# Row sums in two rounded parts, group sums in halves, and the last row tile's closing steps in another order

## The chip, the cores and the metric

The kernel runs on one core of a Trainium2 chip. The core has a matrix engine (TensorE, PE in the profile; its weight loads are PEld), three engines for element-wise work (VectorE or DVE, ScalarE or ACT, GpSimd or POOL) and a queue that issues most of the transfers (SyncE, SP). The metric is the device time of one execution in microseconds, as a median over runs.

## The reference

One layer of a hybrid network on a sequence of 2048 tokens with 1024 features, in float32:

```
mod = silu(c) @ w_ada + b_ada
shift_m, scale_m, gate_m, shift_f, scale_f, gate_f = split(mod, 6)
h = adaln(x, g_norm_mix, shift_m, scale_m)
p = h @ w_in                      # 1024 -> 3592, split into conv, q, k, v, z, a, b
ya = group_rms_norm(gate_b * conv(gate_c * h_conv))       # 8 groups of 64
yb = rms_norm(gated_delta_rule(q, k, v, g, beta)) * silu(z)
x = x + gate_m * (concat(ya, yb) @ w_out)
h = adaln(x, g_norm_ffn, shift_f, scale_f)
gt, up = split(h @ w_gate_up, 2)
x = x + gate_f * ((silu(gt) * up) @ w_down)
shift_o, scale_o = split(silu(c) @ w_ada_final + b_ada_final, 2)
out = adaln(x, g_norm_final, shift_o, scale_o)
```

`adaln(x, gain, shift, scale)` is `rms_norm(x) * gain * (1 + scale) + shift`. `rms_norm` divides by the root of the mean square over the features; the group norm does so over groups of 64.

## The kernel before

**Products in three parts.** To keep float32 accuracy the kernel splits nearly every operand of a matmul into a rounded part (hi, type F32R, "fp32r" in the profile) and the rounded rest (lo), and computes hi·hi, hi·lo and lo·hi into the same bank. These dense matmuls of 128 x 512 are recorded under L322. A weight strip arrives by DMA in a tile `wraw` (a ring of four), ACT casts it to `whi` (L389), DVE subtracts to get `wlo` (L391), and three strips are kept ready ahead. The strip then serves 24 dense matmuls.

**Stages.** The adaLN vectors and the first normalisation come first, then the mixer in four blocks of 512 tokens (from about 133, 400, 640 and 925 us of the span), then the gate and up products (about 1100 to 1950), and then the down products to the end. In each mixer block PE runs the projections, and in between them the small matmuls of the convolutions, of the delta rule and of the norms. These are written as generators, which `dmm` (L322) resumes as the dense matmuls go on.

**PSUM.** Dense results go to a pool `pd` of four banks. All side work takes its bank from another pool of four, `pm`, by `misc_ps()`. A generator that takes a bank before the engines have read its old content makes the next writer wait.

**The order.** A class `Clock` keeps planned times for each engine while the program is built, and decides by them when a generator is resumed. In the mixer it also sorts each engine's queue by the planned begin times and pins that order. So an edit in one place can move instructions in the whole block.

**Rows of adaLN (`to_row`, L502).** A vector such as gate_m is accumulated as products over 128 partitions in `acc`, a tile of the weight ring. The bias is added on DVE (L505), and a matmul with a matrix of ones sums over the partitions and spreads the row to all of them (L510), in halves of 512 columns. In the mixer (`mixing[0]`) this matmul takes `acc` unrounded, in float32; PE needs two passes per half, and the profile counts them as two matmuls. This happens twice: for gate_m in block 0, where `put` copies the half to a tile, and for gate_f in block 2, where `put` copies it on ACT (L498) and stores it by DMA (L499). After the mixer the other branch is used, which rounds first.

**Group sums (`mix_chain`, L1294).** For the group norm the squares of a 128 x 512 tile are split into `sh` and `sl`, and two matmuls with a matrix of group ones (L1307, L1308) sum them in one bank. This happens four times per block, 16 times in all.

**The closing stage (loop over `items`, L1855).** An item is one row tile pair `s` with one group of weights. The down products use Strassen's scheme: per item A11B11, S1T1, A12B21, S2T2 and S4B22, and, in the middle of the next item, the two late products p7 (S3T3) and p4 (A22T4) of the item before. `add` (L1812, DVE) adds a bank to an accumulator of 128 x 1024. With the last group, `finish` (L1815 to L1829) normalises a finished accumulator: `sum_squares` (ACT L536, POOL L530 and L531, a power), then per half a scaling on ACT to a `pm` bank (L1824), a product with go on DVE (L1825), an addition of so on POOL (L1826), and a store (L1829). The last accumulator goes through `finish_last` (L1832 to L1851), which does its halves apart around p4. The names `acc_1_16433`, `acc_0_16478` and `acc_1_16480` below are the second accumulator of the item before the last (row tile 14 in the text on the prediction), and the first and second of the last item. In the new program they are `acc_1_16481`, `acc_0_16526` and `acc_1_16528`.

Of the kernel before, what the change touches and what calls it, by code (L numbers as in the profile page):

```python
# [12 lines left out]
F32 = mybir.dt.float32  # L13
# [197 lines left out]
def layer_kernel(ctx, tc, x, c, w_ada, b_ada, w_ada_final, b_ada_final, g_norm_mix, g_norm_ffn, g_norm_final,  # L211
# [22 lines left out]
    def misc_ps():  # L234
        return pm.tile([P, 512], F32, name="pm")
# [238 lines left out]
    def settled(*tiles):  # L474
        yield
        yield
        while clock.pinned and due(tiles, 0) + 2 > clock.pe:
            yield
# [23 lines left out]
    def to_row(acc, bias_row, put):  # L502
# [1 line left out]
        nc.sync.dma_start(brow, bias_row)  # L504
        nc.vector.tensor_add(acc[0:1, :], acc[0:1, :], brow)  # L505
        if mixing[0]:
            yield from settled(acc)
            for ns in (slice(n * 512, (n + 1) * 512) for n in range(2)):
                ps = misc_ps()
                mm(ps, ones, acc[:, ns], start=True, stop=True)  # L510
                put(ns, ps)
            return
        hi, lo = temp(F32R), []
        clock.kept.add(hi.name)
# [206 lines left out]
    with ExitStack() as actx:  # L721
# [144 lines left out]
        for b in range(NB):  # L866
# [428 lines left out]
            def mix_chain(m, cv):  # L1295
# [8 lines left out]
                nc.vector.tensor_sub(sl, sy, sh.bitcast(F32))  # L1304
                yield sh, sl
                ps = misc_ps()
                mm(ps, gones_r, sh, start=True, stop=False)  # L1307
                mm(ps, gones_r, sl, start=False, stop=True)  # L1308
                give("lv", 2)
                nc.scalar.activation(sy, ps, AF.Sqrt, scale=1.0 / 64, bias=epsc)  # L1310
                nc.vector.reciprocal(sy, sy)
# [499 lines left out]
    def add(s, u, ns, ps):  # L1811
        nc.vector.tensor_add(accs[s, u][:, ns], accs[s, u][:, ns], ps)  # L1812

    def row(s, u):
        r = s // CH * 8 + u * CH + s % CH  # L1815
        return slice(r * P, (r + 1) * P)
# [12 lines left out]
        nc.sync.dma_start(out[row(s, u), :], t)  # L1829


    def finish_last(s, u):  # L1832
        a, go, so = accs[s, u], fin["go_d"], fin["so_d"]
        m = dp.tile([P, D], F32, name="T")[:, h0]
        s2 = [g0.tile([P, 1], F32, name="ss", bufs=4) for _ in range(2)]
        junk = sp.tile([P, D], mybir.dt.bfloat16, name="ht", bufs=2)
        nc.scalar.activation(junk[:, h1], a[:, h1], AF.Square, accum_out=s2[1])
        nc.gpsimd.tensor_mul(a[:, h1], a[:, h1], go[:, h1])  # L1838
        nc.vector.tensor_scalar(s2[1], s2[1], 1.0 / D, EPS, op0=ALU.mult, op1=ALU.add)
        yield  # L1840
        nc.scalar.activation(junk[:, h0], a[:, h0], AF.Square, accum_out=s2[0])
        nc.vector.tensor_mul(m, a[:, h0], go[:, h0])
        nc.vector.scalar_tensor_tensor(s2[0], s2[0], 1.0 / D, s2[1], op0=ALU.mult, op1=ALU.add)
        nc.gpsimd.tensor_tensor(s2[0], s2[0], mhalf[:, :1], op=ALU.pow)
        c0, c1 = slice(0, 256), slice(256, 512)
        nc.scalar.activation(a[:, c1], m[:, c1], AF.Identity, scale=s2[0])
        nc.gpsimd.tensor_add(a[:, c1], a[:, c1], so[:, c1])
        nc.vector.scalar_tensor_tensor(a[:, h1], a[:, h1], s2[0], so[:, h1], op0=ALU.mult, op1=ALU.add)  # L1848
        nc.vector.scalar_tensor_tensor(a[:, c0], m[:, c0], s2[0], so[:, c0], op0=ALU.mult, op1=ALU.add)
        for h in (h1, h0):  # L1850
            nc.sync.dma_start(out[row(s, u), h], a[:, h])  # L1851

    load_pair(1)
    late = None
    for n, (g, s) in enumerate(items):  # L1855
# [33 lines left out]
        next(ahead, None)  # L1889
        dproduct(b, parts("A12", "B21"), True)  # L1890
        add(s, 0, h0, b)
        work()
        dproduct(a, parts("S2", "T2"), False)
        add(s, 0, h1, a)
# [2 lines left out]
        dproduct(c_, parts("S4", "B22"), False)  # L1897
        add(s, 0, h1, c_)
        work()
        if g == last:  # L1900
            spawn(finish(s, 0), 1)
        if late:
            late[1]()
        work()

# [4 lines left out]
        def p4(a=a, s=s, q=parts("A22", "T4"), g=g):  # L1910
            dproduct(a, q, False)
            add(s, 1, h0, a)
            if g == last and s < 2 * CH - 1:
                spawn(finish(s, 1), 1)

        late = p7, p4
    late[0]()
    end = finish_last(2 * CH - 1, 1)
    next(end)
    late[1]()  # L1920
    for _ in end:
        pass
    drain()


# [18 lines left out]
```

## Time and profile before

| | |
|---|---|
| median of 3 runs | 2406.51 us (2406.47 to 2407.99) |
| span of the profiled execution | 2404.1 us |
| the profiled execution's own time | no other than its span |
| mean granted TensorE clock | 0.993 |
| PE / DVE / ACT / POOL busy | 97% / 74% / 44% / 24% |
| HBM traffic | 142 GB/s |

All of the profile is of one execution, and times in it count from the start of its span. A row of an engine's timeline gives start, duration, engine, line and operation, output <- inputs, the shape, and how many instructions the row joins; in square brackets stands the idle time just before it, with what ended it. Consecutive matmuls overlap in such rows, so the cost of one is read from start to start. In the busy times by stretch the granted clock is a share of full speed. Of the waits, a row says which line waited for which, with the sum, the count and the longest.

### The profile page before, as it was taken

To read this page: it belongs to the slowest core of one execution; us is meant where nothing else is said; L and a number is where in the kernel's file an instruction comes from. 1 tells how busy PE (TensorE), PEld (TensorE's weight loads), DVE (VectorE), ACT (ScalarE), POOL (GpSimd) and SP (SyncE) were. 2 spreads that over 40 slices of the span, in tenths; PEclk is the share of its full clock that TensorE was granted. 3 is DMA by queue.
4 is the path that set the end of the run, shared out by engine and by line. 5 is a ranking of instruction groups with operands and counts; after the bars stand their busy time and mean duration, and the time that the engine had idled before them with its cause. 6 is when DMAs were issued, how large, how long until landed. Compare 5 with 4: busy or idle time off the path is not lost. (4 is left out here: it accounts for less than half of the span.)

```text
span 2404.1 us, 30949 instructions
## 1 busy us (share of the span) xinstructions
PE 2342.0 (97%) x11285; PEld 1938.6 (81%) x11285; DVE 1779.7 (74%) x2667; ACT 1050.3 (44%) x1787; POOL 572.9 (24%) x646
## 2 busy tenths in 40 slices
PE   7899999999999999999999999999999999999997
PEld 6788888887788888887888888878888877887786
DVE  5898879775977678788666556875656568878987
ACT  3644664444634564356543334433333323322345
POOL 0241344033513161111000000000000036434448
PEclk9999999999999999999999999999999999999999
DMA  7443565535553345255663334753433374333443
GB/s 252 119 119 92 169 191 164 148 106 166 145 141 122 115 141 146 61 155 161 215 209 116 101 104 122 247 161 90 129 99 105 104 247 154 121 108 119 136 138 142
DMA packets 400992, 341.19 MB, mean 142 GB/s; under 512 B 39796, under 2 KB 343165, under 8 KB 400775
## 3 DMA queue, kind: packets, MB, share of 16 engines
q1 hardware_dynamic: 399430, 337.01, 45.9%
q0 software_dynamic: 1152, 2.10, 0.6%
q8 instruction: 88, 1.44, 0.2%
q14 instruction: 66, 0.53, 0.1%
q10 hardware_dynamic: 256, 0.10, 0.0%
HBM read 265.74 MB, written 75.51 MB: 142 GB/s over the span
## 5 line engine op out<-in xcount | busy, mean ns | idle before, releaser
L389 ACT CAST whi<-wraw 128x1024 fp32r<-128x1024 f32 x286 | 299.7, 1049 | 394.1 <-PE pd L322 170.6
L391 DVE TENSOR_TENSOR wlo<-wraw,whi 128x1024 fp32r<-128x1024 f32 x286 | 360.3, 1261 | 102.7 <-ACT whi L389 100.0
L322 PE MATMUL pd<-hTh,whi 128*128 128x512 f32 x888 | 362.0, 409 | 0.6 <-ACT hTh L564 0.6
L322 PE MATMUL pd<-hTh,wlo 128*128 128x512 f32 x888 | 348.4, 392 | 1.0 <-DVE wlo L391 1.0
L322 PE MATMUL pd<-hTl,whi 128*128 128x512 f32 x888 | 348.2, 392 | 0.1
L322 PEld LDWEIGHTS pd<-hTh,wlo 128*128 128x128 f32 x888 | 167.7, 189 | 38.2 <-DVE wlo L391 1.4
L322 PEld LDWEIGHTS pd<-hTh,whi 128*128 128x128 f32 x888 | 168.5, 190 | 33.6 <-issue 1.0
L322 PEld LDWEIGHTS pd<-hTl,whi 128*128 128x128 f32 x888 | 168.3, 190 | 32.1 <-issue 1.0
L1606 POOL TENSOR_TENSOR wraw<-wraw 128x1024 f32<-128x1024 f32 x2 | 4.9, 2458 | 776.0 <-DMA wraw<-in_w_down_dram 776.0
L1554 DVE TENSOR_TENSOR sg<-sg,pd 128x512 f32<-128x512 f32 x44 | 30.2, 686 | 163.1 <-PE pd L322 163.1
L1812 DVE TENSOR_TENSOR acc<-acc,pd 128x512 f32<-128x512 f32 x192 | 127.3, 679 | 24.6 <-PE pd L322 23.8
L1692 ACT CAST xh<-ra 128x640 fp32r<-128x640 f32 (+1 forms) x85 | 60.4, 722 | 183.0 <-PE pm L322 137.3
L1239 DVE SCALAR_TENSOR_TENSOR cv<-pd,pcb,cv 128x511 f32<-128x511 f32 (+2 forms) x173 | 129.4, 748 | 5.2
L1701 POOL TENSOR_TENSOR xl<-ra,xh 128x640 fp32r<-128x640 f32 (+1 forms) x37 | 62.7, 1695 | 143.9 <-ACT xh L1692 133.7
L1812 DVE TENSOR_TENSOR acc<-acc,pm 128x512 f32<-128x512 f32 x120 | 81.6, 680 | 17.7 <-PE pm L322 17.2
L322 PE MATMUL pd<-whi,ym 128*128 128x512 f32 x256 | 84.8, 396 | 0.0
L1741 POOL TENSOR_TENSOR wraw<-wraw 128x512 f32<-128x512 f32 x40 | 68.8, 1743 | 47.1 <-DMA wraw<-in_w_down_dram 39.7
L322 PE MATMUL pd<-A22h,whi 128*128 128x512 f32 x176 | 68.9, 391 | 3.0 <-DVE sg L1554 3.0
L322 PE MATMUL pm<-S4h,whi 128*128 128x512 f32 x176 | 68.6, 390 | 1.4 <-ACT sg L1548 1.4
L322 PE MATMUL pd<-S2h,whi 128*128 128x512 f32 x176 | 68.6, 390 | 1.0 <-ACT whi L389 1.0
L322 PE MATMUL pd<-S2h,wlo 128*128 128x512 f32 x176 | 68.6, 390 | 0.5 <-DVE wlo L391 0.5
L322 PE MATMUL pd<-S3h,t3h 128*128 128x512 f32 x176 | 69.0, 392 | 0.0
(459 smaller groups left out, 6207.2 us busy)
## 6 DMA issues: line engine op xcount, KB each, us to landing
wraw<-in_w_in_dram SPq DMA_DIRECT2D x112, 512.0 KB, 4.6
wraw<-in_w_gate_up_dram SPq DMA_DIRECT2D x88, 512.0 KB, 3.9
ra<-act SPq DMA_DIRECT2D x80, 448.0 KB, 3.6
wraw<-in_w_out_dram SPq DMA_DIRECT2D x40, 512.0 KB, 3.6
act<-S SPq DMA_DIRECT2D x80, 256.0 KB, 3.5
act<-act SPq DMA_DIRECT2D x68, 256.0 KB, 2.7
wraw<-in_w_ada_dram SPq DMA_DIRECT2D x32, 512.0 KB, 4.2
wraw<-in_w_down_dram SPq DMA_DIRECT2D x22, 512.0 KB, 4.3
```

Source lines behind the costliest of these rows:

```text
L322: mm(*args, **kw)
L389: nc.scalar.copy(hi, raw)
L391: (lo_engines.popleft() if lo_engines else nc.vector).tensor_sub(lo, raw, hi.bitcast(F32))
L1239: nc.vector.scalar_tensor_tensor(cv[:, n - t:], u[:, :BLK - n + t], taps[t], cv[:, n - t:], op0=ALU.mult, op1=ALU.add)
L1554: nc.vector.tensor_add(s5[i], s5[i], a[i])
L1606: nc.gpsimd.tensor_mul(r, r, first_w["gate"])
L1692: nc.scalar.copy(hi, raw[:, c0:c1, :])
L1701: eng.tensor_sub(lo, raw, hi.bitcast(F32))
L1741: nc.gpsimd.tensor_mul(r[:, hs], r[:, hs], gate_f[:, hs])
L1812: nc.vector.tensor_add(accs[s, u][:, ns], accs[s, u][:, ns], ps)
```

## The change

It has three parts.

1. In `to_row` in the mixer, each half of `acc` is split into hi and lo (a cast on ACT, a subtraction on DVE, both into a new tile `both` from the weight ring). Two rounded matmuls sum them into one bank. A `yield` ahead of each half lets the planner put the halves apart.
2. In `mix_chain` the two matmuls of 512 columns become four of 256, in the same bank.
3. In the last item, p4 of the item before comes directly behind A12B21, and its `finish` is begun there. `finish_last` now writes out by hand the closing steps of both accumulators of the last item, and the rest of the `finish` of row tile 14, in one order. For the last accumulator the product with go is on DVE in place of POOL, and the last step is done in one piece of 512 columns on DVE in place of two of 256 on three engines. The two last rows are stored in four halves, one of them issued by ACT.

```diff
         if mixing[0]:
-            yield from settled(acc)
             for ns in (slice(n * 512, (n + 1) * 512) for n in range(2)):
+                yield
+                both = temp(F32R)
+                clock.kept.add(both.name)
+                hi, lo = both[:, :BLK], both[:, BLK:]
+                nc.scalar.copy(hi, acc[:, ns])
+                nc.vector.tensor_sub(lo, acc[:, ns], hi.bitcast(F32))
+                yield from settled(hi, lo)
                 ps = misc_ps()
-                mm(ps, ones, acc[:, ns], start=True, stop=True)
+                mm(ps, ones_r, hi, start=True, stop=False)
+                mm(ps, ones_r, lo, start=False, stop=True)
                 put(ns, ps)
+                clock.kept.discard(both.name)
+                del both, hi, lo
             return
...
                 ps = misc_ps()
-                mm(ps, gones_r, sh, start=True, stop=False)
-                mm(ps, gones_r, sl, start=False, stop=True)
+                for t2 in (slice(0, 256), slice(256, 512)):
+                    mm(ps[:, t2], gones_r, sh[:, t2], start=(t2.start == 0), stop=False, skip_group_check=True)
+                    mm(ps[:, t2], gones_r, sl[:, t2], start=False, stop=(t2.start > 0), skip_group_check=True)
...
-    def finish_last(s, u):
-        a, go, so = accs[s, u], fin["go_d"], fin["so_d"]
+    def finish_last(s, p7, p4, before):
+        t, a, go, so = accs[s, 0], accs[s, 1], fin["go_d"], fin["so_d"]
...
+        next(before)
+        ss = sum_squares(t)
+        p7()
+        next(before)
         nc.scalar.activation(junk[:, h1], a[:, h1], AF.Square, accum_out=s2[1])
-        nc.gpsimd.tensor_mul(a[:, h1], a[:, h1], go[:, h1])
+        nc.vector.tensor_mul(a[:, h1], a[:, h1], go[:, h1])
         nc.vector.tensor_scalar(s2[1], s2[1], 1.0 / D, EPS, op0=ALU.mult, op1=ALU.add)
-        yield
+        for _ in before:
+            pass
+        ps = {h: misc_ps() for h in (h0, h1)}
+        for h in (h0, h1):
+            nc.scalar.activation(ps[h], t[:, h], AF.Identity, scale=ss)
+        p4()
         nc.scalar.activation(junk[:, h0], a[:, h0], AF.Square, accum_out=s2[0])
         nc.vector.tensor_mul(m, a[:, h0], go[:, h0])
+        nc.vector.tensor_mul(t[:, h0], ps[h0], go[:, h0])
         nc.vector.scalar_tensor_tensor(s2[0], s2[0], 1.0 / D, s2[1], op0=ALU.mult, op1=ALU.add)
         nc.gpsimd.tensor_tensor(s2[0], s2[0], mhalf[:, :1], op=ALU.pow)
-        c0, c1 = slice(0, 256), slice(256, 512)
-        nc.scalar.activation(a[:, c1], m[:, c1], AF.Identity, scale=s2[0])
-        nc.gpsimd.tensor_add(a[:, c1], a[:, c1], so[:, c1])
+        nc.vector.tensor_mul(t[:, h1], ps[h1], go[:, h1])
+        nc.gpsimd.tensor_add(t[:, h0], t[:, h0], so[:, h0])
         nc.vector.scalar_tensor_tensor(a[:, h1], a[:, h1], s2[0], so[:, h1], op0=ALU.mult, op1=ALU.add)
-        nc.vector.scalar_tensor_tensor(a[:, c0], m[:, c0], s2[0], so[:, c0], op0=ALU.mult, op1=ALU.add)
-        for h in (h1, h0):
-            nc.sync.dma_start(out[row(s, u), h], a[:, h])
+        nc.sync.dma_start(out[row(s, 1), h1], a[:, h1])
+        nc.sync.dma_start(out[row(s, 0), h0], t[:, h0])
+        nc.vector.scalar_tensor_tensor(a[:, h0], m, s2[0], so[:, h0], op0=ALU.mult, op1=ALU.add)
+        nc.scalar.dma_start(out[row(s, 1), h0], a[:, h0])
+        nc.vector.tensor_add(t[:, h1], t[:, h1], so[:, h1])
+        nc.sync.dma_start(out[row(s, 0), h1], t[:, h1])
...
         dproduct(b, parts("A12", "B21"), True)
         add(s, 0, h0, b)
+        closing = n == len(items) - 1
+        if closing:
+            late[1]()
+            before = finish(s - 1, 1)
+            next(before)
         work()
...
-        if g == last:
+        if g == last and not closing:
             spawn(finish(s, 0), 1)
-        if late:
+        if late and not closing:
             late[1]()
...
-    late[0]()
-    end = finish_last(2 * CH - 1, 1)
-    next(end)
-    late[1]()
-    for _ in end:
-        pass
+    finish_last(2 * CH - 1, *late, before)
```

In mixer block 2 the queue of PE held this around the row sums for gate_f before the change (`kq` and `cv` are tiles of the delta rule and its convolution, `x4` joins four matmuls; the last dense row is followed by 11 more until the next L906):

```order
L322 MATMUL pd<-hTh,wlo 128x512
L906 MATMUL pm<-ck,kq 128x128 x4
L1121 MATMUL pm<-kq 128x128 x4
L906 MATMUL pm<-ck,cv 128x128 x4
L510 MATMUL pm<-wraw,ones_r 128x512 x2
L322 MATMUL pd<-hTh,whi 128x512
```

With the change the same place reads as follows, where L915 and L1130 are the old L906 and L1121:

```order
L322 MATMUL pd<-hTh,wlo 128x512
L915 MATMUL pm<-ck,kq 128x128 x4
L1130 MATMUL pm<-kq 128x128 x4
L915 MATMUL pm<-ck,cv 128x128 x4
L516 MATMUL pm<-wraw,ones_r 128x512
L517 MATMUL pm<-wraw,ones_r 128x512
L322 MATMUL pd<-hTh,whi 128x512
L322 MATMUL pd<-hTl,whi 128x512
```

The two sums of 512 columns stood back to back, each with a bank of its own. Now one sum, of two matmuls, stands there. From it to the next matmul that takes a bank of the side pool are 27 dense matmuls, and the second sum has moved further down.

At the end of the program POOL's queue held this before (so is the `wraw` operand; `ss` are the columns of the norm):

```order
L531 TENSOR_TENSOR ss<-ss,mhalf 128x1
L1826 TENSOR_TENSOR acc_0_16478<-acc_0_16478,wraw 128x512
L1838 TENSOR_TENSOR acc_1_16480<-acc_1_16480,wraw 128x512
L1826 TENSOR_TENSOR acc_0_16478<-acc_0_16478,wraw 128x512
L1826 TENSOR_TENSOR acc_1_16433<-acc_1_16433,wraw 128x512
L1844 TENSOR_TENSOR ss<-ss,mhalf 128x1
L1826 TENSOR_TENSOR acc_1_16433<-acc_1_16433,wraw 128x512
L1847 TENSOR_TENSOR acc_1_16480<-acc_1_16480,wraw 128x256
```

With the change it holds this:

```order
L1836 TENSOR_TENSOR acc_1_16481<-acc_1_16481,wraw 128x512
L539 TENSOR_SCALAR ss<-ss 128x1
L540 TENSOR_TENSOR ss<-ss,mhalf 128x1
L1836 TENSOR_TENSOR acc_1_16481<-acc_1_16481,wraw 128x512
L1868 TENSOR_TENSOR acc_0_16526<-acc_0_16526,wraw 128x512
L1866 TENSOR_TENSOR ss<-ss,mhalf 128x1
```

The last power (L1844, now L1866) had four operations of 512 columns between it and the power ahead of it (L531, now L540), and now has two. What stood behind it on POOL is gone from there.

On DVE the end read as follows before, from the add of p4 of row tile 14:

```order
L1812 TENSOR_TENSOR acc_1_16433<-acc_1_16433,pd 128x512
L1812 TENSOR_TENSOR acc_1_16480<-acc_1_16480,pd 128x512
L1825 TENSOR_TENSOR acc_0_16478<-pm,wraw 128x512
L1839 TENSOR_SCALAR ss<-ss 128x1
L1812 TENSOR_TENSOR acc_1_16480<-acc_1_16480,pd 128x512
L1825 TENSOR_TENSOR acc_0_16478<-pm,wraw 128x512
L1842 TENSOR_TENSOR T<-acc_1_16480,wraw 128x512
L1825 TENSOR_TENSOR acc_1_16433<-pm,wraw 128x512
L1843 SCALAR_TENSOR_TENSOR ss<-ss 128x1
L1825 TENSOR_TENSOR acc_1_16433<-pm,wraw 128x512
L1848 SCALAR_TENSOR_TENSOR acc_1_16480<-acc_1_16480,ss,wraw 128x512
L1849 SCALAR_TENSOR_TENSOR acc_1_16480<-T,ss,wraw 128x256
```

Now it reads, from the first product with go of row tile 14:

```order
L1835 TENSOR_TENSOR acc_1_16481<-pm,wraw 128x512
L1822 TENSOR_TENSOR acc_1_16528<-acc_1_16528,pd 128x512
L1835 TENSOR_TENSOR acc_1_16481<-pm,wraw 128x512
L1854 TENSOR_TENSOR acc_1_16528<-acc_1_16528,wraw 128x512
L1855 TENSOR_SCALAR ss<-ss 128x1
L1822 TENSOR_TENSOR acc_1_16528<-acc_1_16528,pd 128x512
L1864 TENSOR_TENSOR acc_0_16526<-pm,wraw 128x512
L1863 TENSOR_TENSOR T<-acc_1_16528,wraw 128x512
L1865 SCALAR_TENSOR_TENSOR ss<-ss 128x1
L1867 TENSOR_TENSOR acc_0_16526<-pm,wraw 128x512
L1869 SCALAR_TENSOR_TENSOR acc_1_16528<-acc_1_16528,ss,wraw 128x512
L1872 SCALAR_TENSOR_TENSOR acc_1_16528<-T,ss,wraw 128x512
```

The add of p4 of row tile 14 has moved up, ahead of this piece, and the two products of row tile 14 with go, which were near the end, now stand at its start, one of them ahead of the add of the last p7. One more operation (L1874, the addition of so to the second half of `acc_0_16526`) follows the last row.

More of the change, by code (lines that the diff above doesn't have):

```diff
@@ L1912, in p4 @@
             add(s, 1, h0, a)
-            if g == last and s < 2 * CH - 1:
+            if g == last and s < 2 * CH - 2:
                 spawn(finish(s, 1), 1)
         late = p7, p4
-    late[0]()
-    end = finish_last(2 * CH - 1, 1)
-    next(end)
-    late[1]()
-    for _ in end:
-        pass
+    finish_last(2 * CH - 1, *late, before)
     drain()
```

## The prediction

> **What bounds the kernel now.** I read the page first, then the busy times by stretch, then the waits of TensorE, and last the rows around the places that the diff touches.
>
> ```profile
> span 2404.1 us, 30949 instructions
> PE 2342.0 (97%) x11285; PEld 1938.6 (81%) x11285; DVE 1779.7 (74%) x2667; ACT 1050.3 (44%) x1787; POOL 572.9 (24%) x646
> ```
>
> TensorE (PE) is busy for 97% of the span, so a change can gain only where PE stalls, where it works slowly, or after its last matmul. The busy times by stretch (us; busy time and count of PE, PEld, DVE, ACT, POOL; granted clock, DMA share, GB/s) are those of mixer blocks 0, 2 and 3, and of a short piece of block 2:
>
> ```profile
> 133.00:400.00 267.00, 264.57 (x1446) 221.19 (x1445) 225.09 (x368) 140.47 (x286) 98.85 (x125) 1.00 0.49 144
> 640.00:925.00 285.00, 280.07 (x1513) 233.47 (x1513) 216.56 (x373) 146.04 (x301) 102.19 (x136) 0.99 0.47 134
> 925.00:1100.00 175.00, 174.24 (x946) 146.68 (x944) 140.08 (x225) 77.98 (x139) 25.80 (x45) 1.00 0.39 109
> 651.00:665.00 14.00, 10.21 (x40) 7.09 (x39) 13.75 (x24) 8.49 (x18) 4.91 (x7) 0.76 0.59 138
> ```
>
> PE idles 2.43, 4.93 and 0.76 us in these blocks. Of block 2's 4.93, 3.79 lie in the last stretch, where the granted clock also falls to 0.76. The waits of PE (us, times, longest) name that stall:
>
> ```profile
> PE pd L322 <- DVE acc L1812: 7.7, 8, 1.8
> PE pm L510 <- ACT junkd L912: 3.8, 1, 3.8
> ```
>
> L510 is the sum that the diff rewrites. The first row belongs to the down stage, and only its end is touched.
>
> **Part 1, the row in block 2.** PE's rows there, and two of ACT's:
>
> ```profile
> 653.39 1.02 PE L510 MATMUL pm<-wraw,ones_r 128*128 128x512 f32 x2
> 658.20 2.07 PE L510 MATMUL pm<-wraw,ones_r 128*128 128x512 f32 x2 [3.79 <-ACT junkd L912]
> 659.29 1.42 PE L322 MATMUL pd<-hTh,whi 128*128 128x512 f32 x1
> 660.50 0.63 PE L322 MATMUL pd<-hTl,whi 128*128 128x512 f32 x1
> ...
> 664.51 0.60 PE L906 MATMUL pm<-ck,kq 128*128 128x128 f32 x4
> 652.21 0.63 ACT L1277 ACTIVATE cv<-cv 128x512 f32<-128x512 f32 x1 [5.34 <-DVE cv L1241]
> 657.79 0.27 ACT L912 ACTIVATE junkd<-pm 128x128 bf16<-128x128 f32 x1
> ```
>
> Both unrounded sums (two passes each) stand back to back. The first takes the last free bank of the side PSUM pool; the second needs the bank that L906 filled at 651.46, and ACT's L912, which reads that bank, stands behind L1277, itself late by DVE. So PE waits until 658.2. After that it runs slowly: the next matmuls begin 0.43 us apart, not 0.227 (below), until about 663.8.
>
> From 653.39 to 664.51 are 11.12 us, for two sums and 12 dense matmuls. In the new order one sum of two rounded matmuls stands there, and 27 dense matmuls follow before the next matmul into the side pool. They last 27 x 0.227 = 6.1 us, to about 660.0; the bank is read out near 658.1. So the cover is some 1.9 us, and the wait goes. So does the slow stretch, which I take to follow from the idle time: in block 0 the same sums run without a wait, and the clock there stays at 1.00. The price without both is 12 x 0.227 for the dense matmuls and 4 x 0.227 for the two new sums (one of them later): 3.6 us, a gain of 7.5. If only the idle time went, it would be 3.8. The row for the pitch of a dense matmul comes with part 2.
>
> What is late next: DVE, busy 13.75 of 14 us there. The change adds a subtraction on it for each half, as large as an L1812 (0.68, below), and a cast on ACT, half of an L389 (0.5). The casts lie beside PE. Each subtraction delays the DVE conv work queued behind it by up to 0.7, so up to 1.4 in all reaches PE where it waits for DVE; I take 0.5, since PE has some slack at each of its waits. The planner also re-sorts all of block 2 and of block 0, so their small waits are drawn anew. Block 2 has 1.14 us of them now; I take about 2.5, as block 0 has with as full a DVE: +1.35. Together +1.85. Bounds: -1.1 (no wait left) and +4 (one wait of 3.8 more).
>
> **Part 1, the row in block 0.**
>
> ```profile
> 134.07 1.88 PE L510 MATMUL pm<-wraw,ones_r 128*128 128x512 f32 x4
> 136.02 0.40 PE L322 MATMUL pd<-hTl,whi 128*128 128x512 f32 x1
> ```
>
> Between the two stands one dense matmul, so the four passes took 136.02 - 134.07 - 0.23 = 1.72 us. Four rounded matmuls take 4 x 0.227 = 0.91: a gain of 0.8.
>
> **Part 2, the group sums.** PE's rows at one pair of them, and at a run of 128-column matmuls that change weights every time:
>
> ```profile
> 188.03 0.39 PE L1307 MATMUL pm<-lv,gones_r 128*128 128x512 f32 x1
> 188.25 0.39 PE L1308 MATMUL pm<-lv,gones_r 128*128 128x512 f32 x1
> 188.48 0.39 PE L322 MATMUL pd<-hTh,whi 128*128 128x512 f32 x1
> ...
> 204.35 0.39 PE L322 MATMUL pd<-hTh,wlo 128*128 128x512 f32 x1
> 204.57 3.73 PE L1073 MATMUL pm<-lv,ym 128*128 128x128 f32 x32
> 208.06 0.48 PE L322 MATMUL pd<-hTh,whi 128*128 128x512 f32 x1
> ```
>
> From 188.48 to 204.35 are 70 starts of matmuls of 512 columns: 15.87 / 70 = 0.227 us each. The 32 small ones take 3.49 / 32 = 0.109 each. A matmul of 256 columns is not in the trace: it lies between 0.109 and 0.227. Each of the 16 places goes from two at 0.227 (0.454) to four, so to 0.436 at the one end (-0.3 us in all) and 0.908 at the other (+7.3). I take 0.12 each, near the small row, since half the columns of the long row would be 0.113: 16 x (0.48 - 0.454) = +0.4. The Trainium skill's page "TensorE: Matmul & The Clock Gate", section "Back-to-back issue gap", lists 262 cycles for 256 columns and 518 for 512 at 2.4 GHz; by it, as an estimate, 16 x (4 x 0.109 - 2 x 0.216) = +0.1. No run here shows the 256. ACT's reading and all that follows wait for the last of the four, as for the second now.
>
> **Part 3, the end.** DVE, POOL, ACT and PE, in order of time:
>
> ```profile
> 2382.26 0.39 PE L322 MATMUL pd<-whi,xh 128*128 128x512 f32 x1
> 2382.57 0.68 DVE L1812 TENSOR_TENSOR acc<-acc,pd 128x512 f32<-128x512 f32 x1
> 2383.93 3.81 POOL L1826 TENSOR_TENSOR acc<-acc,wraw 128x512 f32<-128x512 f32 x3 [0.50 <-DVE acc L1825]
> 2387.13 1.06 ACT L536 ACTIVATE ht<-acc 128x1024 bf16<-128x1024 f32 x1 [2.55 <-DVE acc L1812]
> 2388.77 0.50 PE L322 MATMUL pd<-whi,yh 128*128 128x512 f32 x1 [0.78 <-DVE acc L1812]
> 2391.77 0.68 DVE L1812 TENSOR_TENSOR acc<-acc,pd 128x512 f32<-128x512 f32 x1
> 2392.96 0.71 DVE L1842 TENSOR_TENSOR T<-acc,wraw 128x512 f32<-128x512 f32 x1
> 2393.08 1.71 POOL L1838 TENSOR_TENSOR acc<-acc,wraw 128x512 f32<-128x512 f32 x1
> 2394.19 0.62 DVE L1843 SCALAR_TENSOR_TENSOR ss<-ss 128x1 f32<-128x1 f32 x1
> 2397.20 0.54 POOL L1844 TENSOR_TENSOR ss<-ss,mhalf 128x1 f32<-128x1 f32 x1
> 2397.77 1.75 DVE L1848 SCALAR_TENSOR_TENSOR acc<-acc,ss,wraw 128x512 f32<-128x512 f32 x1 [2.37 <-POOL ss L1844]
> 2399.44 0.94 DVE L1849 SCALAR_TENSOR_TENSOR acc<-T,ss,wraw 128x256 f32<-128x256 f32 x1
> ```
>
> Now the power (L1844) starts 2.4 us after its input is there, behind POOL's additions, and the last DVE operation ends at 2400.38, 3.72 before the end of the span. In the new order:
>
> - The p4 product of row tile 14 takes the place at 2382.26, and its bank is free when the add at 2382.57 ends, at 2383.25: PE waits 1.0.
> - Its own add ends near 2386.3. The square (1.06 and 0.2) gives 2387.6, POOL is free at 2383.93 + 3.81 = 2387.74, and its two small operations give 2388.6. ACT's scaling and DVE's L1835 (0.7 each, as the adds) reach 2390.0. L1835 stands ahead of the add of the last p7 (to 2390.6), which frees the bank for the last p4: PE starts it at 2390.65, not 2388.77, and ends near 2392.3.
> - The product with go that moves from POOL to DVE (0.7) lies between, beside those six matmuls. The add after them no longer queues behind a square: it ends at 2393.0. Two products with go (0.6 each) and the combine (0.6) end at 2394.8.
> - On POOL the last addition ahead of the power (L1868 in the new code) waits for the first product: it runs from about 2394.0, 1.3 to 1.5 long. The power ends at 2396.0. Three DVE operations of 512 columns, with POOL idle, start 0.6 apart (two of them lie between 2391.77 and 2392.96 now): 2398.0.
>
> The stores in four halves cost nothing here: nothing stands behind them on SP, and ACT, which issues one, has no work left. With the same 3.72 the end is 2401.7: -2.4, bounds -3.5 (the addition slips in earlier) and -0.5 (the three at nearer 1.2 each).
>
> Against it stands a rule of the Trainium skill's page "SBUF — State Buffer", section "SBUF: two separate sides": a DVE operation with two SBUF inputs and a GpSimd operation that reads SBUF take a shared port pair by turns, and the later one blocks fully. The rows agree in part (1.75 at L1848 beside L1826, 1.71 at L1838 beside L1842, which itself took 0.71); by it the addition and the power would end 0.5 to 1.0 later, and this part would give -1.4 to -1.9, inside the bounds above.
>
> **The sum.** -7.5 + 1.85 - 0.8 + 0.4 - 2.4 = -8.45. The profiled execution has no time beside its span of 2404.1, which would become 2395.7. The median of the three runs is 2406.51, 2.4 above that span; shifted by the same sum it is 2398.1.
>
> **Rivals.**
>
> - *The stall comes back elsewhere in a re-sorted block.* For it: DVE is full, the side pool has four banks, and the sums need one each still. Against it: the halves are now apart. It gives back 7.5 us: 2405.6, no difference. Chance 0.14.
> - *A matmul of 256 columns costs as much as one of 512.* Then part 2 is +7.3, not +0.4: 2398.1 + 6.9 = 2405.0, no difference either. Against it: the small ones at 0.109. Chance 0.09.
> - *The weight ring starves (slower).* The accumulator, the hi/lo tile and a normalised row tile hold three of the ring's four slots for longer in block 2:
>
> ```profile
> wraw<-in_w_in_dram SPq DMA_DIRECT2D x112, 512.0 KB, 4.6
> L389 ACT CAST whi<-wraw 128x1024 fp32r<-128x1024 f32 x286 | 299.7, 1049 | 394.1 <-PE pd L322 170.6
> L391 DVE TENSOR_TENSOR wlo<-wraw,whi 128x1024 fp32r<-128x1024 f32 x286 | 360.3, 1261 | 102.7 <-ACT whi L389 100.0
> 675.37 0.60 PE L589 MATMUL pm<-ck,wraw 128*128 128x128 f32 x4
> ```
>
> With one slot a strip needs 4.6 + 1.05 + 1.26 = 6.9 us one after the other, and PE uses it up in 24 x 0.227 = 5.4. Three strips are ready ahead, 16.3 us. It decides when the slots are held for longer than these cover; I count some 12 us, from the second sum's start after 664 to the matmul that reads the normalised tile (its row is 675.37 now). The row's two stores, which wait on SP for ACT's copies ahead of weight loads, have the same cover. Past it, two gaps like that of 658.2, at 7.5 with the slow stretch: +15, 2413. Chance 0.05.
> - That the sums do not speed up (the rounded pair as long as the unrounded) would cost 0.8 twice, inside the range. Other: 0.02. The forecast keeps 0.70.
>
> **How the numbers follow.** The forecast is 2398.1. The low end is 2394.0: the no-wait bound (-3 on the +1.85) and the -3.5 of part 3. The high end, 2405.0, takes in a second drawing of waits, the -0.5 of part 3 and the 256-column rival up to its full price. A measurement of this kernel can tell about 0.2%, 4.8 us, from no change: faster is below 2401.7, slower above 2411.3. Faster is the forecast's 0.70 and 0.02 of the first rival, where the stall that comes back is under 3.6 us. No difference is the other 0.12 of it, 0.09 of the second and 0.01 of the unknown: 0.22. Slower is the ring's 0.05 and 0.01 of the unknown.
>
> **What would show it.** Right: no stall of PE at the new sums near 653 and the clock there at 1.00; about 0.12 from one group-sum matmul to the next; the power of the last row tile near 2395.5 less the earlier gains. Wrong: a stall of over 3 us anywhere in blocks 0 or 2, a pitch of 0.2 in the group sums, or a last p4 that starts more than 3 us later against the product ahead of it.

## The result, and the profile after

The median of eight runs is 2401.20 us, against 2407.61 us for eight runs of the kernel before. The ratio is 0.9971, with a 95% interval of 0.9961 to 0.9981: 7.0 us faster by the ratio, between 4.6 and 9.4; the two medians differ by 6.4. The profiled execution took 2403.85 us, with a span of 2402.1. It is one of the two slowest of the eight, so its span says less than its parts.

The page's first lines, the busy times of the same stretches, and the short piece of block 2:

```profile
span 2402.1 us, 31013 instructions
PE 2341.1 (97%) x11317; PEld 1939.5 (81%) x11317; DVE 1788.3 (74%) x2673; ACT 1051.7 (44%) x1790; POOL 571.4 (24%) x643
```

```profile
133.00:400.00 267.00, 263.66 (x1453) 221.24 (x1452) 229.35 (x372) 142.25 (x289) 99.17 (x127) 1.00 0.51 146
640.00:925.00 285.00, 283.92 (x1552) 237.88 (x1551) 224.78 (x392) 148.78 (x305) 99.80 (x136) 1.00 0.48 139
651.00:665.00 14.00, 13.73 (x74) 11.18 (x73) 13.42 (x24) 8.55 (x23) 3.71 (x6) 1.00 0.58 136
```

PE idles 1.08 us in block 2, not 4.93, and the clock in the short piece is 1.00, not 0.76. The sums stand there without a wait, and dense matmuls follow at once, 0.23 apart:

```profile
652.53 0.49 PE L516 MATMUL pm<-wraw,ones_r 128*128 128x512 f32 x1
652.86 0.39 PE L517 MATMUL pm<-wraw,ones_r 128*128 128x512 f32 x1
653.09 0.39 PE L322 MATMUL pd<-hTh,whi 128*128 128x512 f32 x1
653.32 0.39 PE L322 MATMUL pd<-hTl,whi 128*128 128x512 f32 x1
...
674.90 0.39 PE L516 MATMUL pm<-wraw,ones_r 128*128 128x512 f32 x1
```

Block 0 has more idle time than before, 3.34 instead of 2.43. A part of it is new, at the group sums:

```profile
193.73 0.39 PE L1318 MATMUL pm<-lv,gones_r 128*128 128x256 f32 x1 [1.48 <-DVE lv L1313]
...
222.45 0.28 PE L1317 MATMUL pm<-lv,gones_r 128*128 128x256 f32 x1
222.57 0.28 PE L1318 MATMUL pm<-lv,gones_r 128*128 128x256 f32 x1
222.69 0.28 PE L1317 MATMUL pm<-lv,gones_r 128*128 128x256 f32 x1
222.81 0.28 PE L1318 MATMUL pm<-lv,gones_r 128*128 128x256 f32 x1
222.92 0.40 PE L322 MATMUL pd<-hTh,whi 128*128 128x512 f32 x1
```

Four of 256 columns last 0.47 us (222.45 to 222.92), against 0.45 for the two before. At 193.73 the second matmul waits for the low part, which DVE had not written yet.

At the end, the rows that the prediction walked through:

```profile
2383.47 0.50 PE L322 MATMUL pd<-whi,yh 128*128 128x512 f32 x1 [0.83 <-DVE acc L1822]
2390.91 0.50 PE L322 MATMUL pd<-whi,yh 128*128 128x512 f32 x1 [1.66 <-DVE acc L1822]
2392.61 0.69 DVE L1822 TENSOR_TENSOR acc<-acc,pd 128x512 f32<-128x512 f32 x1
2394.49 1.64 POOL L1868 TENSOR_TENSOR acc<-acc,wraw 128x512 f32<-128x512 f32 x1 [0.29 <-DVE acc L1864]
2396.22 0.55 POOL L1866 TENSOR_TENSOR ss<-ss,mhalf 128x1 f32<-128x1 f32 x1
2396.80 0.75 DVE L1869 SCALAR_TENSOR_TENSOR acc<-acc,ss,wraw 128x512 f32<-128x512 f32 x1
2398.13 0.68 DVE L1874 TENSOR_TENSOR acc<-acc,wraw 128x512 f32<-128x512 f32 x1
```

The power ends at 2396.77 and the last DVE operation at 2398.81, 3.3 us before the end of the span.

To see where the time came from, I read the starts of four matmuls that every profile has: the eight small ones near 102 us that open the delta rule (L1003 before), the first output projection of blocks 1 and 2 (they take `yah`), the first S2 product of the gate and up stage, and the first wait of the down stage (near 1957). The last column runs from the last row near 2268 whose PE wait is for the add (`dh,xh`) to the end. All in us, and each row is one execution; to the right stand the ratio of the times to the kernel before, over all runs, and its 95% interval.

| kernel | blocks 0, 1 | block 2 | block 3 | gate, up | closing | ratio | interval |
|---|---|---|---|---|---|---|---|
| before | 424.4 | 268.5 | 311.1 | 851.2 | 136.2 | | |
| the change | 423.8 | 261.8 | 311.1 | 858.3 | 134.0 | 0.9971 | 0.9961 to 0.9981 |
| the change again | 424.1 | 261.4 | 310.5 | 854.5 | 134.0 | 0.9978 | 0.9968 to 0.9988 |
| row sums alone | 424.7 | 261.8 | 311.0 | 852.0 | 136.4 | 0.9969 | 0.9957 to 0.9981 |
| group sums alone | 424.6 | 267.3 | 310.8 | 855.9 | 138.6 | 1.0011 | 1.0002 to 1.0020 |
| closing alone | 424.8 | 268.6 | 310.7 | 854.1 | 134.0 | 0.9984 | 0.9975 to 0.9993 |
| halves apart, unrounded | 424.7 | 270.1 | 310.8 | 853.6 | 136.1 | 1.0010 | 1.0002 to 1.0019 |
| rounded, halves together | 428.1 | 263.2 | 310.8 | 856.1 | 136.6 | 0.9999 | 0.9990 to 1.0009 |
| parts computed, not used | 424.0 | 262.7 | 311.1 | 854.0 | | 0.9975 | 0.9966 to 0.9984 |

(One cell is empty because that execution has its last such wait at another matmul.) Block 2 gains 6.7 to 7.1 us and the closing steps 2.2. What the profile of the change seems to give back is in the gate and up stage, which the diff doesn't touch, and which takes 851 to 858 us in these executions.

### The profile page after: what moved, and what is told of

Same layout as the page of the kernel before. It is cut to its first block, busy times and chain, and to the rows that moved or that the text cites. A ratio compares the mean times of both kernels' runs of the same rounds, so it can differ in the third digit from the quotient of the medians.

```text
span 2402.1 us, 31013 instructions
## 1 busy us (share of the span) xinstructions
PE 2341.1 (97%) x11317; PEld 1939.5 (81%) x11317; DVE 1788.3 (74%) x2673; ACT 1051.7 (44%) x1790; POOL 571.4 (24%) x643
## 4 chain that ended last, share of the span: by engine, by line
PE 66%; DVE 16%; DMA 7%; ACT 4%; issue 4%; POOL 2%; SPq 0%; ACTq 0%; DVEq 0%; POOLq 0%
PE pd L322 41%; PE pm L322 17%; DVE wlo L391 3%; DVE cv L1248 2%; DVE acc L1822 1%; DMA wraw<-in_w_in_dram 1%; ACT whi L389 1%; DMA y<-xT 1%; DVE wraw L469 1%; POOL wraw L1751 1%; DVE cv L1246 1%; PE pm L1082 1%; DMA A12d<-y 1%; DMA acc<-x 1%; PE pm L1090 1%
## 5 line engine op out<-in xcount | busy, mean ns | idle before, releaser
L322 PE MATMUL pd<-A22l,whi 128*128 128x512 f32 x176 | 69.7, 396 | 0.0
L322 PE MATMUL pd<-A22h,wlo 128*128 128x512 f32 x176 | 69.6, 395 | 0.0
```

Source lines behind the costliest of these rows:

```text
L322: mm(*args, **kw)
```

## The experiments

The main theory is the one of the prediction: the gain in the mixer is the wait for the bank and the slow clock behind it, and both go because the halves of the sums are apart. The rivals to it: the re-sorting through the group sums made the gain, or the fewer passes of the rounded matmuls did. For the gate and up stage, the landing theory holds that what it gives back hangs on how long single stores take to land in one execution; the shift theory, that the earlier end of the mixer brings it about each time.

**The changed kernel again**, with no edit.

> The changed kernel once more, unedited, for a second profile and more times. Landing theory (the 7 us that the changed kernel gives back in the gate and up stage hang on how long single stores take to land, which differs from one execution to the next): the first S2 matmul of the gate and up stage starts near 1099 us again, but the stretch from it to the first closing products differs from that of the first profile by 2 us or more, and the number of PE waits for the DVE addition into sg is not five again. Shift theory (the earlier end of the mixer itself puts stores and loads in each other's way): the same five waits, within half a microsecond each. Time: 2398 to 2404 us either way.

Its 12 runs have a median of 2400.73, against 2407.29 for 29 of before. The gate and up stage took 3.8 us less than in the first profile. Four of the five waits for sg are there again, the fifth (0.44) is not. Two of them have about the same length in both, and what differs is what comes behind them (first the rows of the first profile and of the second, then the busy times of the 5 us from each):

```profile
1235.42 0.50 PE L322 MATMUL pd<-A22h,whi 128*128 128x512 f32 x1 [1.82 <-DVE sg L1564]
1582.89 0.50 PE L322 MATMUL pd<-A22h,whi 128*128 128x512 f32 x1 [1.80 <-DVE sg L1564]
```

```profile
1232.89 0.50 PE L322 MATMUL pd<-A22h,whi 128*128 128x512 f32 x1 [1.85 <-DVE sg L1564]
1579.59 0.50 PE L322 MATMUL pd<-A22h,whi 128*128 128x512 f32 x1 [2.04 <-DVE sg L1564]
```

```profile
1235.42:1240.42 5.00, 5.00 (x15) 3.98 (x16) 2.98 (x4) 0.54 (x1) 0.00 (x0) 0.66 0.82 221
1582.89:1587.89 5.00, 5.00 (x15) 3.96 (x16) 4.22 (x6) 1.10 (x2) 0.00 (x0) 0.66 0.59 182
```

```profile
1232.89:1237.89 5.00, 5.00 (x22) 4.15 (x23) 4.03 (x5) 1.54 (x2) 0.00 (x0) 1.00 0.81 237
1579.59:1584.59 5.00, 5.00 (x22) 4.15 (x23) 4.88 (x6) 1.54 (x2) 0.00 (x0) 1.00 0.63 196
```

15 matmuls in 5 us against 22: seven times 0.227, 1.6 us at each place, or 3.2 of the 3.8. So most of the difference between these two executions of one program in this stage is whether the clock falls after a wait of 1.8 us. The shift theory, which asks for the same loss each time, falls with this. It falls for the waits too: the kernel with the closing steps alone (below), whose mixer is that of before, has waits for sg of 1.11 us at 1198.44 and 1.32 at 1238.77, the places of those near 1193 and 1235 here. The landing theory explains only the waits, not the larger part behind them.

**Row sums alone** (the first part of the change's diff on the kernel before).

> The kernel before with the row sums of the change alone. Main theory (the gain is in the wait for the bank and the slow clock behind it): the first S2 matmul of the gate and up stage starts 7 to 8 us earlier than 1106.6, and the median is 4 to 7.5 us lower than before. Rival (the re-sorting through the group sums made the gain): no more than 3 us in both.

The median is 2400.19, the ratio 0.9969, and block 2 takes 261.8. The first S2 product starts at 1100.6, 6.0 us sooner, or 6.4 counted from the matmuls near 102 us, where 7 to 8 were expected. Most of the mixer's gain comes with this part, so the rival (the group sums' re-sorting) is out.

**Group sums alone** (the second part).

> The kernel before with the group sums in halves of 256 columns alone. Main theory: the four matmuls of a place start 0.11 to 0.125 us apart, so the 16 places cost between -0.2 and +0.4 us together; the stall of 3.8 us at the unrounded row sums stays; the first S2 matmul within 1.5 us of 1106.6 and the time within 2 us of before. Rival (the second matmul of a place now comes sooner and waits for DVE's low part): 1 to 3 us more idle time of PE at those lines than before, and the time 1 to 3 us longer.

The stall at L510 stays, 3.79 us. The mixer is 1.3 us shorter than before, and no new wait over 0.4 us stands at the halves. Yet the median is 2410.34, 2.6 us longer (0.5 to 4.8). The profiled execution has one wait of 4.3 us in the down stage with a slow clock behind it, which the diff does not touch. Its span is 5.8 us longer than that of before: 4.7 lie in the gate and up stage and 3.4 behind it, where no group sum stands, and the rest is shorter. So the time got longer by more than the 2 us that the main theory allowed, and why is open. The rival's waits are not what did it.

**Closing steps alone** (the third part).

> The kernel before with the closing steps of the change alone. Main theory: the mixer as before, with its 3.8 us stall; from the first matmul of the last closing item's sixth product to the end of the span 2 to 2.5 us less than before, and the median 1.5 to 2.5 us lower. Rival (the end is set by the landing of the last store, and the order ahead of it does not matter): within 0.5 us at the end.

2403.92 us, ratio 0.9984, and 134.0 instead of 136.2 us from the last wait near 2268 to the end, as in both profiles of the change. The rival is out: the order ahead of the last store is worth 2.2 us. The median fell by 3.4, more than the 1.5 to 2.5 expected, but the interval (1.7 to 6.0 us) holds the 2.2.

**Halves apart, unrounded.** On the kernel before:

```diff
-            yield from settled(acc)
             for ns in (slice(n * 512, (n + 1) * 512) for n in range(2)):
+                yield
+                yield from settled(acc)
                 ps = misc_ps()
                 mm(ps, ones, acc[:, ns], start=True, stop=True)
```

> The kernel before, its row sums left unrounded, with one yield that lets the planner put the two halves apart. Main theory (the wait for the bank and the slow clock behind it are the gain, and they go because the halves are apart): no stall of PE at the sums near 653 us; from the small matmuls ahead of the first sum to the same point behind it the clock stays at 1.00; the stretch from 108 us to the first S2 matmul of the gate and up stage is 5 to 7 us shorter than the 998 of before; time 4 to 7 us lower. Rival (the rounded matmuls made it, by fewer passes): the stretch shrinks by less than 2 us, with a stall or a slow clock at each unrounded sum.

The stall at the sum is gone, and the clock is full behind it. But the time is not lower (2410.99 us, ratio 1.0010), and block 2 is 1.6 us longer than before. PE's rows at the sum and some 55 us later, and DVE's at that second place, with the busy times there; last, the rows of DVE and PE at that second place in the kernel before:

```profile
651.05 1.02 PE L511 MATMUL pm<-wraw,ones_r 128*128 128x512 f32 x2
651.51 0.79 PE L322 MATMUL pd<-hTh,whi 128*128 128x512 f32 x1
652.14 0.39 PE L322 MATMUL pd<-hTl,whi 128*128 128x512 f32 x1
...
705.61 1.70 PE L1074 MATMUL pm<-lv,ym 128*128 128x128 f32 x8 [2.44 <-DVE lv L1068]
707.91 5.26 PE L1074 MATMUL pm<-lv,ym 128*128 128x128 f32 x24 [0.61 <-DVE lv L1068]
704.75 0.71 DVE L1068 STREAM_TRANSPOSE lv<-X 128x512 f32<-128x512 f32 x1 [8.28 <-POOL X L1050]
```

```profile
704.00:714.00 10.00, 7.79 (x38) 7.42 (x39) 8.31 (x15) 2.34 (x4) 1.75 (x3) 0.66 0.17 48
```

```profile
706.61 0.71 DVE L1067 STREAM_TRANSPOSE lv<-X 128x512 f32<-128x512 f32 x1 [3.18 <-POOL X L1049]
709.27 3.73 PE L1073 MATMUL pm<-lv,ym 128*128 128x128 f32 x32
```

L1074 is the delta rule's product of transposed tiles. Its data comes through a store and a load of `dx`, POOL's L1050 and DVE's transposes. Before, these transposes began at 706.61 and PE came to the matmuls at 709.27, without a wait. Here they begin 1.9 us sooner, but PE is there 6.1 us sooner (705.61 less the wait of 2.44): the stall at the sums had hidden the chain. Now PE waits 3.05 us in two steps, and 24 matmuls take 5.26 us, twice the 0.109 each of before, at a mean clock of 0.66 over these 10 us. So the main theory's first half holds (halves apart, no wait, full clock), and its second half falls: that alone gains nothing. The pass theory doesn't follow from this: behind the unrounded sum the clock is full.

**Rounded, halves together.** The split of both halves first, then all four matmuls:

```diff
+            for ns in halves:
+                both = temp(F32R)
...
+            yield from settled(*(t for p in pairs for t in p[:2]))
+            for ns, (hi, lo, both) in zip(halves, pairs):
+                ps = misc_ps()
+                mm(ps, ones_r, hi, start=True, stop=False)
+                mm(ps, ones_r, lo, start=False, stop=True)
```

> The kernel before, its row sums rounded as in the change, but both halves split first and all four matmuls issued together. Main theory: the four passes that are saved per row (0.8 us in each of two rows) are all that the rounding gives by itself, so 1.6 us, unless the later place of the sums, 12 rows further down in the order, frees the bank: then there is no stall of 3 us near 653 either and the gain is 5 to 7. Rival (unrounded matmuls slow the clock for those behind them): the slow stretch of 0.43 us per dense matmul is gone even if a stall of over 2 us stays.

Also no gain: 2406.16, ratio 0.9999. Block 2 takes 263.2, so the stall went with the sums' later place; but blocks 0 and 1 take 3.7 us more than before. In the order that the planner made here, waits stand there that the kernel before does not have:

```profile
274.13 0.79 PE L322 MATMUL pd<-wlo,ym 128*128 128x512 f32 x1 [3.14 <-DVE wlo L391]
456.98 0.51 PE L1319 MATMUL pm<-lv,gones_r 128*128 128x512 f32 x1 [3.36 <-ACT lv L1315]
```

The first is all new: DVE's subtraction for that strip starts at 272.86, behind a reciprocal of 3.35 us (from 267.31) and three more operations. The second is 1.0 longer than the 2.35 of before. The expectation left out that another block can pay.

**Parts computed, not used.** The row sums of the change, cast and subtraction included, but with the old matmul. The rounded parts are not used:

```diff
-                mm(ps, ones_r, hi, start=True, stop=False)
-                mm(ps, ones_r, lo, start=False, stop=True)
+                mm(ps, ones, acc[:, ns], start=True, stop=True)
```

> The kernel before with the row sums of the change, cast and subtraction and all, except that the matmul still takes the unrounded accumulator: the rounded parts are computed and not used. Order theory (the halves apart remove the wait, and the added ACT and DVE work makes the planner put the delta rule's matmuls L1082 in block 2 some 40 rows of PE's queue further down, where their data is in time; the faster passes are a small matter): the stretch between the first output projections of blocks 1 and 2 is 262 to 264 us, as with the rounded sums, and the time 4 to 7 us below before. Pass theory (the rounded matmuls make the difference between a gain of 7 and none): the stretch is 268 or more, with a stall of over 1 us or a clock below 0.9 near 705.

2399.62 us, ratio 0.9975 (0.9966 to 0.9984), block 2 at 262.7. The order theory holds. The unrounded sums run without a wait, and the delta rule's product comes at 713.24, with its data there:

```profile
652.79 1.12 PE L516 MATMUL pm<-wraw,ones_r 128*128 128x512 f32 x2
674.40 1.02 PE L516 MATMUL pm<-wraw,ones_r 128*128 128x512 f32 x2
713.24 3.74 PE L1081 MATMUL pm<-lv,ym 128*128 128x128 f32 x32
```

In PE's queue that product stands 283 matmuls behind the first sum here, 242 behind it in the kernel with the halves merely apart, and 239 in the kernel before. So the gain in block 2 needs the added work on ACT and DVE, and not its result. That this work acts by making the planner move those matmuls down is read from these rows; no run pins the new order without the work, so that step is argued and not tried by itself. What the rounded matmuls add can't be told: 262.7 here lies among the 261.4 to 263.0 of the seven profiles with the row sums of the change.

**Without the group sums in halves** (the change with the two old matmuls of 512 columns).

> The change without its second part: the group sums in two matmuls of 512 columns. If the halves of 256 columns cost what the kernel with them alone suggests, the median is 2 to 3 us below that of the change, about 2398. If the 16 places cost nothing, as their rows show (0.11 to 0.12 us from one to the next), it is within 1 us of the change, and the stretch from 108 us to the first S2 matmul is within 1 us of its 990.

2397.70 us, ratio 0.9963 (0.9949 to 0.9976). From the matmuls near 102 to the first S2 product are 995.7 us, against 996.6 and 996.0 in the change. The median is 3.0 us below that of the change in its later runs (2400.73), but the intervals overlap.

**The difference for gate and up into another tile**, in the changed kernel and in the kernel before:

```diff
-            nc.vector.tensor_sub(t5, t5, t2)
-            put("S4", t5)
+            nc.vector.tensor_sub(t2, t5, t2)
+            put("S4", t2)
```

> The changed kernel with one more edit: the last difference of the sums for the gate and up stage is written into the tile of S2, stored long before, in place of the tile of A12, whose store has just been issued. Landing theory (DVE waits there for a store to land, 12 to 19 us in all, and the addition into sg behind it keeps PE waiting): DVE's idle time at that line falls below 6 us, the waits of PE for sg near 1193 and 1235 go, and the stretch from the first S2 matmul to the first closing products is 2 to 4 us shorter than the 854 to 858 of the other profiles of the changed mixer; time 1 to 4 us below the changed kernel. Shift theory: another wait takes their place, the stretch stays above 854.

> The kernel before with the difference for the gate and up stage written into the tile of S2. Landing theory: DVE's waits for the store of A12 belong to both kernels, so the waits of PE for sg near 1200 and 1240 are gone here as well, and the median is 0 to 3 us lower than before. Shift theory (only the changed kernel has them): no difference, since the profile of before shows PE waits for sg at two later places only.

The wait went as expected. DVE's group at that line in the change, then in the edited change (the last two figures are the idle time before it and what ended it):

```profile
L721 DVE TENSOR_TENSOR y<-y 128x512 f32<-128x512 f32 x4 | 2.8, 692 | 18.7 <-DMA A12d<-y 18.7
```

```profile
L721 DVE TENSOR_TENSOR y<-y 128x512 f32<-128x512 f32 x4 | 2.8, 692 | 5.3 <-ACT y L618 5.3
```

PE's waits for sg near 1193 and 1235 went with it in the change (the profile of before had none there), and a wait of 1.8 us for ACT's L1550 came at 1186.68. The stage took 853.3 there, just under the 854 above which the shift theory put it, and 850.6 in the edited kernel before. The times: 2398.56, ratio 0.9967 (0.9955 to 0.9979), with an interval that overlaps that of the change; and 2407.41, 1.0006 (0.9998 to 1.0015). So DVE's wait exists in both kernels (14.7 us in before), and taking it away is worth nothing that these runs can tell (the two kernels below, which have the edit too, take 854.5 and 855.0 for the stage). The landing theory names a real wait, not the cause of a measured time.

**All that pointed upwards together**: without the halves of group sums, with the edit above, and with the add of the last p7 put ahead of the products of row tile 14 by added order edges on DVE; and the same with the halves.

```diff
-        next(before)
         ss = sum_squares(t)
         p7()
         next(before)
+        next(before)
+        for i, j in zip(dve, dve[1:]):
+            tc.add_manual_dep(j, i.name, edge, reason="order")
```

> The change without the group sums in halves, with the difference for the gate and up stage written into the tile of S2, and with the add of the last p7 put ahead of the two products with go of row tile 14 on DVE. Landing theory: the waits for sg near 1193 and 1235 gone, so 1 to 3 us below the change without group sums, 2395 to 2397. The last edit: PE starts the last p4 0.8 us sooner against the product ahead of it; the end gains up to 0.8 if that product sets it and nothing if ACT's scaling of the last row tile but one sets it.

> The same with the group sums in halves of 256 columns: the second comparison of the group sums. If they cost 2 to 3 us, as the two earlier pairs of medians have it, the median is that much higher than that of the kernel without; if they cost nothing, as the rows of the mixer have it, within 1 us.

2400.11 us, ratio 0.9975 (0.9964 to 0.9985), where 2395 to 2397 was expected, and with the halves 2399.21, 0.9968 (0.9956 to 0.9980). Here the halves look cheaper, not dearer, so the cost seen in the kernel with them alone stays unsettled: 2.6 us against before, 3.0 against the change without them, and -0.9 here. Neither kernel is clearly faster than the change. The last edit did start the last p4 0.9 us sooner, counted from the last wait near 2268, but the closing took 134.4 and not 134.0. DVE and POOL there:

```profile
2389.57 1.73 DVE L1869 TENSOR_TENSOR T<-acc,wraw 128x512 f32<-128x512 f32 x1
2387.94 2.81 POOL L1835 TENSOR_TENSOR acc<-acc,wraw 128x512 f32<-128x512 f32 x2
```

The product that now comes sooner takes 1.73 us beside POOL's additions, where the same product in the change took 0.68. This fits the rule on the shared port pair that the prediction weighed (the Trainium skill's page "SBUF — State Buffer", section "SBUF: two separate sides").

## Why the prediction was right, and where not

It gave 2398.1 in a range of 2394.0 to 2405.0, and faster; measured are 2401.2 and -6.4 us between medians, where the sum had -8.45. The number came out partly by luck: the gain of the largest term depends on the planner's new order, which the prediction did not work out.

- **Row in block 2** (-7.5 and +1.85, so -5.65): -6.7 to -7.1 measured. Both causes are confirmed: no wait, full clock. But the step from "the wait goes" to "the time goes" failed as a reason. With the halves merely apart the wait goes as the prediction says, and a stall of the first rival's kind takes its place at the delta rule's product. Against that rival the prediction had set that the halves are apart, and that was no protection. What let the gain through, as far as the rows tell, is the re-sorting, which the prediction entered as a draw of small waits at +1.35 (block 2 idles 1.08 us, where 2.5 was taken). It was the larger lever: with the sums unrounded and apart, +1.6 in block 2 with one order, -5.8 with another.
- **The slow stretch follows the idle time, not the unrounded sums**: right. The unrounded sums at 651.05 and 652.79 have a full clock behind them.
- **Row in block 0** (-0.8): not to be seen in the stage. The rounded sums start 0.23 us apart there as well, but blocks 0 and 1 together are only 0.6 and 0.2 us shorter in the two profiles of the change, and 0.3 longer with the row sums alone. In the change, the wait at the group sum (1.48) is larger than what was to be gained.
- **Group sums** (+0.4): the matmuls cost 0.117 each, as taken: 16 x (0.47 - 0.45) = 0.3. The Trainium skill's page "TensorE: Matmul & The Clock Gate", section "Back-to-back issue gap", lists 262 cycles for 256 columns, an estimate of 0.109 at 2.4 GHz; the row has 0.117. The wait at 193.73 was not in the sum, which had the four matmuls end like the two. With this part alone the median rose by 3.1 (2.6 by the ratio), of all terms the one furthest from its forecast; what the runs measure beyond the rows is open, as the later pairs disagree.
- **The end** (-2.4): -2.2, in three profiles. Of the steps, PE waited 0.83 where 1.0 was taken. From the wait near 2268 the last p4 starts at 122.8, and 122.8 was worked out (2390.65 less 2267.85). The power ended 0.5 us later than worked out: L1868 began 0.2 later and took 1.64 beside DVE, where 1.3 to 1.5 was taken. The landing behind the last operation was 3.3 instead of 3.72, which made that good by luck. A longer L1868 is what the rule would give that the prediction set against its sum (the Trainium skill's page "SBUF — State Buffer", section "SBUF: two separate sides").
- **The sum against the median.** From the matmuls near 102 us to the first S2 product and at the end, the two profiles of the change gain 9.6 and 10.2 us against that of before, and the medians moved by 6.4. The profile of before has the shortest gate and up stage of the nine in the table, 851.2 us, where their mean is 854.4. The shift of the sum from one execution to a median took no account of this. (Every run with a span on record takes 1.7 to 2.0 us more than its span. So the profiled execution of before does have time beside its span, contrary to the table of its profile, and most of the 2.4 us between its span and the median is that. The sum is not touched by it.) By medians the three parts alone gave -7.1, +3.1 and -3.4, so -7.4 together against the -6.4 of the change. The rest of the difference is not settled; the group sums may be in it.
- **The slower rival** (the weight ring) did not come: the page of the profile after has 0.0 us of idle time ahead of the dense matmuls with `wlo`.

## What to carry to other kernels

A wait that is removed pays only if whatever comes next on that engine has its data by then; follow PE's queue to the next matmul whose input crosses a DMA, and compare the two times, before entering a gain. Where a planner sorts the program, an edit is worth what its new order is worth, so try the same edit with the work kept and the result thrown away: it tells order from work. And read a gain of a few microseconds by stage, over several profiles, since one execution of the same program differs from the next by as much.

## What was not expected of the hardware

How long PE must idle before its clock falls is no fixed number here. The same wait of 1.53 us at 62 us, ahead of any changed code, has a clock of 1.00 over the next 5 us in one kernel's execution and 0.66 in another's (halves apart; parts computed, not used):

```profile
61.44:66.44 5.00, 4.91 (x23) 3.29 (x24) 3.88 (x7) 1.93 (x8) 0.73 (x3) 1.00 0.00 0
```

```profile
62.27:67.27 5.00, 5.00 (x17) 3.12 (x18) 2.75 (x5) 0.76 (x3) 0.25 (x1) 0.66 0.00 0
```

In the nine profiles of the table I counted the PE waits of over 1.4 us after the first 60 us. The clock over the 5 us behind them was under 0.9 for 18 of the 47 under 2.5 us, and for all 13 of 2.5 us or more. The Trainium skill's page "TensorE: Matmul & The Clock Gate", section "What's actually happening", puts the fall after an idle window of about 3.4 us that runs freely. A window that runs freely would make the fall a matter of chance, as seen, but here it came behind 1.53 us.

In the traces' record of the granted clock every fall lasts one or two steps of 3.41 us at half the clock: in the kernel before it is 0.50 from 62.95 to 66.36 us and from 656.86 to 663.69. So a step costs at most 1.7 us; in the two pairs from the changed kernel (its second run, above) a fall cost 1.6. From 60 us to about 2380 the nine executions have between 2 and 7 such steps, which is up to 3.4 to 12 us each. By that estimate the falls can make up much of the spread of 5 to 12 us between the runs of one kernel. The 195 runs that list their clock agree in sign: within a series longer runs have the lower mean clock (correlation -0.59 over all, each series taken from its own mean). This was not tried by itself.
